# A decoder layer in split fp32: the gate's steps over four blocks, gate rows unsplit, the second norm by a diagonal, the up pass tile by tile

## The chip, the cores and the metric

One core of a Trainium2 chip runs the whole program. The time is device microseconds of one execution; lower is better. TensorE (PE) multiplies matrices, VectorE (DVE) and ScalarE (ACT) work elementwise, GpSimd (POOL) fills buffers and issues some DMAs, SyncE (SP) issues the weights' DMAs.

## The reference, cut to what matters

One layer for 256 tokens of width 2048, all in float32. The vector `c` gives six rows or columns of modulation by a 2048 x 12288 product.

```python
mod = (c_act @ w_mod[l] + b_mod[l])[:, None, :]
sh_m, sc_m, g_m, sh_f, sc_f, g_f = jnp.split(mod, 6, axis=-1)
h = rmsnorm(x, mix_pre_w[l]) * (1 + sc_m) + sh_m
y = hybrid_mixer(h, w_in[l], conv_w[l], gate_w2[l], gate_b[l], gla_norm_w[l], w_out[l])
x = x + g_m * rmsnorm(y, mix_post_w[l])
h = rmsnorm(x, ffn_pre_w[l]) * (1 + sc_f) + sh_f
y = conv_ffn(h, w_up[l], ffn_conv_w[l], w_down[l])
x = x + g_f * rmsnorm(y, ffn_post_w[l])
```

The mixer projects `h`, runs a short convolution and a gated linear attention whose decay is `log_sigmoid((a_lr @ gate_w2 + gate_b)) / 16`, summed along the tokens of each chunk of 64, and projects back. `conv_ffn` is an up product to 11264 columns, a convolution along tokens, `silu(g) * val`, and a down product.

## The kernel before

Float32 products are made from two fp32r halves. For each unit of weights (mostly 1 MB) SP issues a DMA into `raw`; ACT casts it to the high half `wh` (`high`, L141); DVE subtracts to get the low half `wl` (`low`, L146). PE does three products: high by high, high weights by low activations, low weights by high activations. There are six `raw` buffers and three each of `wh` and `wl`. Each of the four stages is a list of such units: in-projection (`tail` is its last chunk of 18 units and what follows), out-projection (`owait`), up pass (`s1`, then `s2`), down pass.

`drive` writes all of them out in one order. Each unit has lists of other steps: `early`, then the DMA and cast of the unit two ahead and the low half of the next, then `pre`, the matmuls, `mid`, the finishing steps of the unit before, and `late`. Every engine executes its own part strictly in that order, so a step that waits holds up all behind it on its engine. `hold` moves the cast and the low half of a unit. PSUM has eight banks, given out in the order of release.

Modulation sums are made on DVE step by step (`macc`, L137): one step stands in most units. Then 128-row sums are added up by products with ones: columns (L285) for the norms, rows (L308, L309) for the gates. `split_acc` (L265, L267) first makes high and low halves of the sums in a `wh` and a `wl` buffer; where it is left out the product is true fp32, which PE executes as two instructions.

- Gate chain: `gla_gate0` to `gla_gate2` make the gate's product, absolute value, exponential, logarithm (ACT, L537 to L539), minimum (DVE, L137 on `big`) and the running sums (four scans, L547), placed at `tail[0]` and `tail[1]`.
- Second norm (`second_norm`, `norm_part0`): after the residual, x is scaled by 1/rms on DVE (`scale_part`, L1135, 256, 256 and 512 columns), turned by transposes on PE (L348), scaled and shifted by the modulation (L354, first tile L1150 and L1151), and split into high (L363) and low (L367) as `h2[0]` to `h2[3]`, two k-blocks each. `h2[4]` to `h2[7]` follow within the up pass.
- Up pass: a group is 512 of the 11264 columns, four column tiles in four PSUM banks. `s1` takes k-blocks 0 to 7 of ten groups (20 units of four k-blocks), `s2` the rest: k 8 to 15 of these ten and all of the other twelve (68 units). In a unit the loop over k is outside and that over column tiles inside; each step is a pair of matmuls of 512 and 256 columns (L874, L876). The first two k-blocks of the first unit are done apart (L868). Finished groups are copied by ACT (L797) and summed by DVE (L799).
- The second modulation's sums `f2` are split at `s1[13]`, its products stand at `s1[14]` and `s1[15]`.

Of the kernel before, what the change touches and what calls it, by code (L numbers as in the profile page):

```python
# [34 lines left out]
LWS = 1  # L35
ORD = (0, 5, 1, 6, 2, 7, 3, 8, 4, 9, 10)
# [7 lines left out]
F2_AT = (70, 74, 13)  # L44
# [25 lines left out]
def drive(units):  # L70
# [5 lines left out]
    for i, u in enumerate(units):  # L76
        for f in u.early:
            f()
        if not u.hold:
            if i + 2 < n:  # L80
                units[i + 2].prep()
            if i + 1 < n:
                units[i + 1].low()
        elif u.hold == 1:
            units[i + 1].low()
# [5 lines left out]
        if u.hold:  # L91
# [13 lines left out]
def layer_kernel(ctx: ExitStack, tc, x, c, w_mod, b_mod, mix_pre_w, mix_post_w, w_in, conv_w, gate_w2, gate_b,  # L105
# [187 lines left out]
    def mod_rows(accs, post, tiles):  # L293
# [240 lines left out]
    def gla_gate1():  # L534
# [186 lines left out]
    def z_part(t, n, ps):  # L721
# [4 lines left out]
        square_sum(ps, ssy[t][:, n:n + 1])  # L726
# [9 lines left out]
    def out_units(nh):  # L736
# [7 lines left out]
        def unit(k2):  # L744
# [24 lines left out]
            def fin(ts=(0, 1), ns=(0, 1)):  # L769
                for t in ts:  # L770
                    for n in ns:
                        z_part(t, nh * 2 + n, pss[t, n])
# [67 lines left out]
    def up_units(og, ks, mode):  # L840
# [4 lines left out]
        def unit(k0):  # L845
# [11 lines left out]
            def mm():  # L857
# [5 lines left out]
                if apart:  # L863
                    for i in range(3):
                        for kk in range(2):
                            for o in range(4):
                                w, xl, half = ((wh, 0, 0), (wh, 1, 1), (wl, 0, 1))[i]
# [28 lines left out]
    def down_unit(k):  # L896
# [49 lines left out]
        def fin():  # L946
            for t in range(2):
                zs[t][0] = zs[t][1] = None
            for t in range(2):
                for n in range(4):  # L950
                    z_part(t, n, down["ps"][t, n])
# [66 lines left out]
    owait[r0 + R0].late.append(lambda: split_acc(gacc))  # L1018
# [16 lines left out]
    tail[1].early.append(gla_gate1)  # L1035
    tail[1].late.append(gla_gate2)
# [37 lines left out]
    for g in ORD:  # L1074
        for og in (g, g + 11):
            s2 += up_units(og, range(8, 16), "rest") if og in A else up_units(og, range(16), "all")
# [3 lines left out]
    def second_norm():  # L1080
# [13 lines left out]

        products()
# [11 lines left out]
        scale_part(0, 0, r0)  # L1107
        st_f["ps"] = [turn_norm(hx, (k, k + 1), None, (0,)) for k in range(0, 8, 2)]
        r1 = rstd_of(sums[1], 4, "n21")
        scale_part(1, 0, r1)  # L1110
        columns()
        st_f["r"] = [r0, r1]

    def put_away():
        for t in range(2):
            for h in range(2):
                if h:
                    scale_part(t, 1, st_f["r"][t])
# [9 lines left out]
    def scale_part(t, h, r):  # L1128
# [121 lines left out]
```

## Time and profile before

| | |
|---|---|
| Time, median of 3 (lowest to highest) | 1223.4 us (1222.33 to 1223.87) |
| The profiled execution's own time | 1223.4 us |
| Its span | 1221.5 us |
| PE, DVE, ACT busy | 96%, 78%, 47% |
| Mean granted TensorE clock | 0.989 of full speed |
| DMA traffic over the span | 262 GB/s |

The span runs from the first to the last record of the profile. "Busy" adds up the time in which an engine executes. PEclk is the TensorE clock that was granted, 1.00 for its full 2.4 GHz and 0.50 for 1.2 GHz. An entry such as [2.28 <-DVE wl L146] says that the engine was idle for 2.28 us before and what ended this. In a matmul's row `128*128` is the weights' size; the first matmul of a fenced row with a count stands for a run of like ones.

### The profile page before, as it was taken

The page shows a single profiled execution, that of the slowest core. Times are in us where ns is not written, and L with a number is a line of the kernel's source. Part 1 is how long each engine was busy: PE and PEld are TensorE (multiplying, and loading weights), DVE is VectorE, ACT ScalarE, POOL GpSimd, SP SyncE. Part 2 cuts the span into 40 slices and gives each one's busy share as a digit, 9 for nine tenths or more (in the row PEclk, how much of TensorE's full clock was granted, in tenths as well). Part 3 has the DMA queues.
Part 4 walks back from the last instruction along what each step waited for, and adds up shares of the span by engine and source line. Part 5 has one row for each costly group of instructions (what it writes and reads, how often), then busy time and mean ns, then how long its engine had stood idle before and what let it go on. Part 6 is the DMA issues. An engine that isn't in the chain of part 4 may idle for free.

```text
span 1221.5 us, 17082 instructions
## 1 busy us (share of the span) xinstructions
PE 1174.3 (96%) x6977; PEld 1043.0 (85%) x6977; DVE 955.2 (78%) x973; ACT 572.9 (47%) x668; POOL 31.7 (3%) x49
## 2 busy tenths in 40 slices
PE   2999999999999998999999999999999999999997
PEld 1999999989997787888888888888888888888885
DVE  5999999989998879974787979798885665444464
ACT  5553432443565437444554555454545543433441
POOL 2000020000001001000000000000000000000000
PEclk9999999999999998998999999999999999999999
DMA  9999999987599995995575776758664665555522
GB/s 306 386 390 385 311 358 394 397 284 254 190 324 347 336 343 205 383 360 169 180 268 202 250 277 208 275 206 278 239 234 150 249 246 189 207 178 201 195 81 69
DMA packets 128046, 320.73 MB, mean 263 GB/s; under 512 B 8341, under 2 KB 35685, under 8 KB 118240
## 3 DMA queue, kind: packets, MB, share of 16 engines
q1 hardware_dynamic: 125360, 312.63, 71.9%
q0 software_dynamic: 2320, 6.94, 1.6%
q8 instruction: 55, 0.90, 0.3%
q14 instruction: 23, 0.19, 0.0%
q10 hardware_dynamic: 288, 0.07, 0.0%
HBM read 315.42 MB, written 4.19 MB: 262 GB/s over the span
## 4 chain that ended last, share of the span: by engine, by line
PE 54%; DVE 0%; ACT 0%; DVEq 0%; issue 0%; ACTq 0%
PE ps L874 22%; PE ps L876 11%; PE ps L733 7%; PE ps L734 7%; PE ps L732 7%; PE ps L285 0%; DVE big L137 0%; PE ps L348 0%; PE ps L308 0%; PE ps L309 0%; ACT junk L335 0%; DVE big L727 0%; DVEq L1234 0%; DVE big L799 0%; ACT rz L321 0%
## 5 line engine op out<-in xcount | busy, mean ns | idle before, releaser
L141 ACT CAST wh<-raw 128x2048 fp32r<-128x2048 f32 (+3 forms) x202 | 366.2, 1816 | 500.2 <-PE ps L874 163.5
L146 DVE TENSOR_TENSOR wl<-raw,wh 128x2048 fp32r<-128x2048 f32 (+3 forms) x202 | 437.7, 2168 | 137.1 <-ACT wh L141 137.1
L874 PE MATMUL ps<-big,wh 128*128 128x512 f32 x1400 | 490.2, 394 | 0.0
L876 PE MATMUL ps<-big,wl 128*128 128x256 f32 x1400 | 393.3, 281 | 0.0
L874 PEld LDWEIGHTS ps<-big,wh 128*128 128x128 f32 x1400 | 263.4, 188 | 59.3
L876 PEld LDWEIGHTS ps<-big,wl 128*128 128x128 f32 x1400 | 265.8, 190 | 0.0
L479 PE MATMUL ps<-big,wl 128*128 128x256 f32 x733 | 210.7, 287 | 4.6 <-DVE wl L146 4.6
L477 PE MATMUL ps<-big,wh 128*128 128x256 f32 x733 | 211.9, 289 | 0.2 <-ACT wh L141 0.2
L478 PE MATMUL ps<-big,wh 128*128 128x256 f32 x733 | 209.9, 286 | 0.0
L137 DVE SCALAR_TENSOR_TENSOR macc<-raw,c_act,macc 128x2048 f32<-128x2048 f32 (+1 forms) x96 | 199.4, 2077 | 3.7 <-DMA raw<-in_w_mod_dram 3.6
L733 PE MATMUL ps<-wl,big 128*128 128x512 f32 x456 | 177.8, 390 | 3.6 <-DVE wl L146 3.6
L732 PE MATMUL ps<-wh,big 128*128 128x512 f32 x456 | 177.9, 390 | 0.0
L734 PE MATMUL ps<-wh,big 128*128 128x512 f32 x456 | 177.5, 389 | 0.0
L479 PEld LDWEIGHTS ps<-big,wl 128*128 128x128 f32 x733 | 143.1, 195 | 5.8 <-DVE wl L146 5.7
L477 PEld LDWEIGHTS ps<-big,wh 128*128 128x128 f32 x733 | 143.4, 196 | 2.7 <-PE ps L423 1.3
L478 PEld LDWEIGHTS ps<-big,wh 128*128 128x128 f32 x733 | 143.3, 196 | 0.1
L733 PEld LDWEIGHTS ps<-wl,big 128*128 128x128 f32 x456 | 85.6, 188 | 22.4 <-DVE wl L146 4.8
L732 PEld LDWEIGHTS ps<-wh,big 128*128 128x128 f32 x456 | 85.6, 188 | 17.8
L734 PEld LDWEIGHTS ps<-wh,big 128*128 128x128 f32 x456 | 85.6, 188 | 17.6
L137 DVE SCALAR_TENSOR_TENSOR big<-big,fcw,big 128x254 f32<-128x254 f32 (+1 forms) x176 | 72.2, 479 | 0.0
L799 DVE TENSOR_TENSOR big<-big,ps 128x256 f32<-128x256 f32 x88 | 31.1, 416 | 43.5 <-ACT big L797 43.5
L819 ACT ACTIVATE big<-big,fcw 128x256 f32<-128x256 f32 x88 | 37.8, 512 | 14.1 <-DVE big L810 14.1
(183 smaller groups left out, 686.9 us busy)
## 6 DMA issues: line engine op xcount, KB each, us to landing
raw<-in_w_up_dram SPq DMA_DIRECT2D x88, 1024.0 KB, 5.3
raw<-in_w_mod_dram SPq DMA_DIRECT2D x64, 1024.0 KB, 7.1
raw<-in_w_down_dram SPq DMA_DIRECT2D x44, 1024.0 KB, 4.8
raw<-in_w_in_dram SPq DMA_DIRECT2D x24, 960.0 KB, 8.3
raw<-in_w_mod_dram SPq DMA_DIRECT2D x32, 640.0 KB, 7.8
raw<-in_w_out_dram SPq DMA_DIRECT2D x16, 1024.0 KB, 7.0
raw<-in_w_in_dram SPq DMA_DIRECT2D x12, 1024.0 KB, 8.0
raw<-in_w_mod_dram SPq DMA_DIRECT2D x22, 512.0 KB, 6.7
```

The costliest lines, as they stand in the source:

```text
L137: nc.vector.scalar_tensor_tensor(o, a, s, b, op0=op0, op1=op1)
L141: nc.scalar.copy(hi, raw)
L146: nc.vector.tensor_sub(lo, raw, hi.bitcast(F32))
L477: nc.tensor.matmul(ps, w[0][:, kk, cs], ht[:, k % 2, 0, :], start=st, stop=False)
L478: nc.tensor.matmul(ps, w[0][:, kk, cs], ht[:, k % 2, 1, :], start=False, stop=False)
L479: nc.tensor.matmul(ps, w[1][:, kk, cs], ht[:, k % 2, 0, :], start=False, stop=sp)
L732: nc.tensor.matmul(ps, a[:, i, 0, ts_], w[0][:, kk, ns], start=st, stop=False)
L733: nc.tensor.matmul(ps, a[:, i, 0, ts_], w[1][:, kk, ns], start=False, stop=False)
L734: nc.tensor.matmul(ps, a[:, i, 1, ts_], w[0][:, kk, ns], start=False, stop=sp)
L819: nc.scalar.activation(st["c"][:, o, :], st["u"][o], AF.Copy, scale=fcw[:, 2, ch + o:ch + o + 1])
L874: nc.tensor.matmul(pss[o], wh[:, kk, cs], h2[k // 2][:, k % 2, :, :], start=(first and kk == 0), stop=False)
L876: nc.tensor.matmul(pss[o][:, 1, :], wl[:, kk, cs], h2[k // 2][:, k % 2, 0, :], start=False, stop=(last and kk == 3))
```

## The change

- The gate's steps become `gla_gate0` to `gla_gate4` and are spread from `tail[0]` to `tail[3]`: the exponential at the end of `tail[1]`, the logarithm at the start of `tail[2]`, the minimum at its end, the scans at the start of `tail[3]`.
- The first gate's sums (`gacc`) and `f2` are no longer split; their products are true fp32. `split_acc` remains for the second gate.
- The first half of x is no longer scaled. DVE multiplies the identity by 1/rms (`diagonal`), and PE multiplies x by it (`turn_scaled`), in true fp32. The last quarter's second half is turned behind the first up unit's matmuls; the second up unit's cast and low half stand behind the first two quarters.
- In a unit of the up pass the loop over column tiles is outside, that over k inside. `apart` takes high, low weights, low activations. `s2` begins with a whole group (5), and the order of groups is written out.
- `f2`'s steps reach `s1[15]`, its products stand at `s1[16]` and `s1[17]`; `h2[4]` to `h2[7]` are turned from `s1[17]` to `s2[1]`.
- The squares and the products with the gate's row of an out tile take turns between two banks.

```diff
-LWS = 1
-ORD = (0, 5, 1, 6, 2, 7, 3, 8, 4, 9, 10)
+ORD = (5, 0, 11, 16, 1, 12, 6, 17, 2, 13, 7, 18, 3, 14, 8, 19, 4, 15, 9, 20, 10, 21)
...
-            hi, lo = accs[1]
+            terms, r = (accs[1], ones_r) if len(accs) == 2 else ((accs[0],), ones)
             for q in range(2):
                 s, cs = slice(q * 512, (q + 1) * 512), slice(h * 1024 + q * 512, h * 1024 + (q + 1) * 512)
                 ps = bank([P, 512])
-                nc.tensor.matmul(ps, ones_r, hi[:, cs], start=True, stop=False)
-                nc.tensor.matmul(ps, ones_r, lo[:, cs], start=False, stop=True)
+                for j, term in enumerate(terms):
+                    nc.tensor.matmul(ps, r, term[:, cs], start=j == 0, stop=j == len(terms) - 1)
                 nc.vector.tensor_mul(parts[h][:, s], ps, parts[h][:, s])
...
         nc.scalar.activation(kb, qb, AF.Exp, scale=-1.0)
+
+    def gla_gate2():
+        qb, kb = gla["qk"]
         nc.scalar.activation(qb, kb, AF.Ln, bias=ones[:, 0:1])
 
-    def gla_gate2():
-        b, (qb, kb) = gla["b"], gla["qk"]
+    def gla_gate3():
+        qb, kb = gla["qk"]
         for hh, ps in enumerate(gla["z"]):
             hs = slice(hh * 2, hh * 2 + 2)
             stt(kb[:, hs, :], ps, 0.0, qb[:, hs, :], ALU.min, ALU.subtract)
+
+    def gla_gate4():
+        b, (qb, kb) = gla["b"], gla["qk"]
         for h in range(HEADS):
...
-                for kk in range(2 * apart, 4):
-                    k = k0 + kk
-                    for o in range(4):
+                for o in range(4):
+                    for kk in range(2 * apart, 4):
+                        k = k0 + kk
...
-    owait[r0 + R0].late.append(lambda: split_acc(gacc))
...
-    tail[1].early.append(gla_gate1)
-    tail[1].late.append(gla_gate2)
+    tail[1].late.append(gla_gate1)
+    tail[2].early.append(gla_gate2)
+    tail[2].late.append(gla_gate3)
+    tail[3].pre.append(gla_gate4)
...
+        def diagonal(t, r):
+
+            if t == 0:
+                st_f["dg"] = slot([P, 2, P])
+            st_f["d", t] = d = st_f["dg"][:, t, :]
+            nc.vector.tensor_scalar_mul(d, ident, r)
...
-        scale_part(0, 0, r0)
-        st_f["ps"] = [turn_norm(hx, (k, k + 1), None, (0,)) for k in range(0, 8, 2)]
+        diagonal(0, r0)
+        columns()
+        st_f["ps"] = [bank([P, 2, T]) for _ in range(4)]
+        for j in range(4):
+            turn_scaled(j, 0)
         r1 = rstd_of(sums[1], 4, "n21")
-        scale_part(1, 0, r1)
-        columns()
+        diagonal(1, r1)
         st_f["r"] = [r0, r1]
+
+    def turn_scaled(j, t):
+        for i in range(2):
+            k = j * 2 + i
+            nc.tensor.matmul(st_f["ps"][j][:, i, t * P:(t + 1) * P], xs[t][0][:, k * P:(k + 1) * P], st_f["d", t],
+                             start=True, stop=True)
...
     def norm_part0():
-        for j in range(4):
-            turned(0, j)
-            used(0, j)
-            if j == LWS:
-                s1[1].low()
-
-    owait[-1].hold, s1[0].hold = 1, 2
+        for j in range(3):
+            turn_scaled(j, 1)
+        used(0, 0)
+        used(0, 1)
+        s1[1].prep()
+        s1[1].low()
+        used(0, 2)
+
+    def norm_part1():
+        turn_scaled(3, 1)
+        used(0, 3)
+
+    owait[-1].hold, s1[0].hold = 3, 2
...
+    s1[0].mid.append(norm_part1)
...
-    s1[13].late.append(lambda: split_acc(f2))
-    s1[14].late.append(lambda: f_products(0))
-    s1[15].mid.append(lambda: f_products(1))
-    s1[15].mid.append(lambda: later["c"][2]())
-    for j in range(4):
-        at = 16 + 2 * (j // 2)
-        s1[at].late.append(lambda j=j: turned(1, j))
-        s1[at + 1].pre.append(lambda j=j: used(1, j))
+    s1[16].late.append(lambda: f_products(0))
+    s1[17].mid.append(lambda: f_products(1))
+    s1[17].mid.append(lambda: later["c"][2]())
+    for j, u in enumerate((s1[18], s1[19], s2[0], s2[1])):
+        (s1[17].late if j == 0 else u.early).append(lambda j=j: turned(j))
+        u.pre.append(lambda j=j: used(1, j))
```

DVE around the gate, before. `macc` is a modulation step, `big_2600` the gate's minimum, L547 the scans, `wl` the low halves of the coming blocks:

```order
L137 SCALAR_TENSOR_TENSOR macc_1922<-raw_2607,c_act,macc_1922 128x2048
L146 TENSOR_TENSOR wl_2618<-raw_2543,wh_2545 128x1920
L137 SCALAR_TENSOR_TENSOR big_296<-ps_2549,big_296 128x512
L137 SCALAR_TENSOR_TENSOR big_2600<-ps_2601,big_2599 128x512
L137 SCALAR_TENSOR_TENSOR big_2600<-ps_2604,big_2599 128x512
L547 SCALAR_TENSOR_TENSOR big_2598<-reset,big_2600 128x256 x4
L137 SCALAR_TENSOR_TENSOR macc_1922<-raw_2673,c_act,macc_1922 128x2048
L146 TENSOR_TENSOR wl_2680<-raw_2614,wh_2616 128x1920
```

DVE at the same place in the changed kernel:

```order
L136 SCALAR_TENSOR_TENSOR macc_1922<-raw_2607,c_act,macc_1922 128x2048
L145 TENSOR_TENSOR wl_2614<-raw_2543,wh_2545 128x1920
L136 SCALAR_TENSOR_TENSOR big_296<-ps_2549,big_296 128x512
L136 SCALAR_TENSOR_TENSOR macc_1922<-raw_2666,c_act,macc_1922 128x2048
L145 TENSOR_TENSOR wl_2674<-raw_2610,wh_2612 128x1920
L136 SCALAR_TENSOR_TENSOR big_296<-ps_2580,big_296 128x512
L402 TENSOR_TENSOR big_335<-big_335,ps_2631 128x512
L136 SCALAR_TENSOR_TENSOR big_2600<-ps_2601,big_2599 128x512
L136 SCALAR_TENSOR_TENSOR big_2600<-ps_2604,big_2599 128x512
L136 SCALAR_TENSOR_TENSOR macc_1922<-raw_2727,c_act,macc_1922 128x2048
L145 TENSOR_TENSOR wl_2732<-raw_2670,wh_2672 128x1280
L552 SCALAR_TENSOR_TENSOR big_2598<-reset,big_2600 128x256 x4
```

A modulation step and a low half (`wl_2674`) now stand ahead of the minimum steps, and one more of each ahead of the scans.

ACT around the second modulation sums, before: L141 casts weights, L265 casts the sums, L797 copies a finished group out of its banks:

```order
L141 CAST wh_5056<-raw_5054 128x2048
L265 CAST wh_5092<-macc_4094 128x1024 x2
L141 CAST wh_5100<-raw_5098 128x2048
L797 COPY big_5140<-ps_5009 128x256
L797 COPY big_5140<-ps_5010 128x256
L797 COPY big_5140<-ps_5011 128x256
L797 COPY big_5140<-ps_5012 128x256
```

ACT at the products' new place in the changed kernel (L140 casts weights, L805 copies):

```order
L140 CAST wh_5132<-raw_5130 128x2048
L140 CAST wh_5170<-raw_5168 128x2048
L805 COPY big_5210<-ps_5082 128x256
L805 COPY big_5210<-ps_5083 128x256
L805 COPY big_5210<-ps_5084 128x256
L805 COPY big_5210<-ps_5085 128x256
L140 CAST wh_5231<-raw_5229 128x2048
```

No cast of sums stands between the weights' casts and the copies.

PE from the end of the first up unit to the second, before. `ps_4424` to `ps_4427` are the four banks, `big_4403` is `h2[1]`, `big_4413` `h2[2]`, `wh_4387` the second unit's weights:

```order
L874 MATMUL ps_4426<-big_4403,wh_4231 128x512
L876 MATMUL ps_4426<-big_4403,wl_4247 128x256
L874 MATMUL ps_4427<-big_4403,wh_4231 128x512
L876 MATMUL ps_4427<-big_4403,wl_4247 128x256
L874 MATMUL ps_4424<-big_4413,wh_4387 128x512
L876 MATMUL ps_4424<-big_4413,wl_4406 128x256
L874 MATMUL ps_4425<-big_4413,wh_4387 128x512
L876 MATMUL ps_4425<-big_4413,wl_4406 128x256
L874 MATMUL ps_4426<-big_4413,wh_4387 128x512
L876 MATMUL ps_4426<-big_4413,wl_4406 128x256
```

PE at the same place in the changed kernel, where `big_4400` is `h2[2]` and `big_4452` `h2[3]`:

```order
L882 MATMUL ps_4406<-big_4388,wh_4223 128x512
L884 MATMUL ps_4406<-big_4388,wl_4239 128x256
L882 MATMUL ps_4406<-big_4388,wh_4223 128x512
L884 MATMUL ps_4406<-big_4388,wl_4239 128x256
L1135 MATMUL ps_4357<-big_4350,big_3947 128x128 x2
L882 MATMUL ps_4403<-big_4400,wh_4393 128x512
L884 MATMUL ps_4403<-big_4400,wl_4395 128x256
L882 MATMUL ps_4403<-big_4400,wh_4393 128x512
L884 MATMUL ps_4403<-big_4400,wl_4395 128x256
L882 MATMUL ps_4403<-big_4452,wh_4393 128x512
L884 MATMUL ps_4403<-big_4452,wl_4395 128x256
```

The turning of the last quarter stands between the units, and the first bank takes `h2[3]` after two pairs, where before all four banks took `h2[2]` first.

## Rows read from the trace of the kernel before

**Rows 1.** The page, part 1: busy us (share of the span) xinstructions of each engine.
```profile
PE 1174.3 (96%) x6977; PEld 1043.0 (85%) x6977; DVE 955.2 (78%) x973; ACT 572.9 (47%) x668; POOL 31.7 (3%) x49
```

**Rows 2.** Windows: us, busy us (xinstructions) of five engines, PEclk, DMA share, GB/s.
```profile
251.28:262.18 10.90, 10.90 (x91) 10.90 (x91) 7.61 (x9) 8.22 (x7) 0.00 (x0) 1.00 0.59 210
262.18:271.61 9.43, 7.15 (x48) 6.95 (x46) 9.43 (x8) 1.81 (x1) 0.00 (x0) 0.82 0.82 278
457.15:481.14 23.99, 20.90 (x121) 18.38 (x120) 20.98 (x30) 19.10 (x35) 3.84 (x5) 0.79 0.45 161
481.14:548.98 67.84, 67.84 (x386) 58.80 (x385) 58.02 (x47) 29.49 (x36) 0.00 (x0) 1.00 1.01 375
554.80:568.14 13.34, 10.61 (x49) 9.51 (x49) 3.62 (x5) 2.95 (x5) 0.00 (x0) 0.74 0.67 225
644.00:710.56 66.56, 66.56 (x386) 58.69 (x385) 58.67 (x75) 33.47 (x38) 0.00 (x0) 1.00 0.72 251
```

**Rows 3.** Timeline, gate chain: start us, us, engine, operation, count [idle before <-releaser].
```profile
256.86 1.29 DVE L137 SCALAR_TENSOR_TENSOR big<-ps,big 128x512 f32<-128x512 f32 x2 [3.29 <-ACT big L539]
...
262.65 2.15 DVE L146 TENSOR_TENSOR wl<-raw,wh 128x1920 fp32r<-128x1920 f32 x1
...
264.86 0.43 PE L479 MATMUL ps<-big,wl 128*128 128x256 f32 x1 [2.28 <-DVE wl L146]
```

**Rows 4.** Timeline, out-projection around the gate rows.
```profile
381.98 1.91 ACT L141 CAST wh<-raw 128x2048 fp32r<-128x2048 f32 x1
...
386.04 1.91 ACT L265 CAST wh<-macc 128x2048 fp32r<-128x2048 f32 x1 [2.15 <-issue]
...
387.99 2.29 DVE L267 TENSOR_TENSOR wl<-macc,wh 128x2048 fp32r<-128x2048 f32 x1 [3.82 <-ACT wh L265]
...
391.24 0.39 PE L308 MATMUL ps<-wh,ones_r 128*128 128x512 f32 x1
...
393.11 0.40 PE L732 MATMUL ps<-wh,big 128*128 128x512 f32 x1
393.24 2.29 DVE L146 TENSOR_TENSOR wl<-raw,wh 128x2048 fp32r<-128x2048 f32 x1
395.58 0.50 PE L733 MATMUL ps<-wl,big 128*128 128x512 f32 x1 [2.08 <-DVE wl L146]
...
405.24 0.50 PE L733 MATMUL ps<-wl,big 128*128 128x512 f32 x1 [1.16 <-DVE wl L146]
```

**Rows 5.** Timeline, PE alone: fp32 matmuls of 128 and 256 columns.
```profile
305.11 1.95 PE L566 MATMUL ps<-big 128*128 128x128 f32 x16
306.89 6.64 PE L474 MATMUL ps<-hf,raw 128*128 128x256 f32 x30
313.37 1.95 PE L566 MATMUL ps<-big 128*128 128x128 f32 x16
```

**Rows 6.** Timeline, second norm, DVE, GpSimd (POOL) and ACT.
```profile
462.40 3.07 DVE L1135 TENSOR_SCALAR big<-big,n 128x256 f32<-128x256 f32 x3
...
463.10 1.82 POOL L171 MEMSET macc<- 128x2048 f32 x1
...
466.09 1.01 DVE L1135 TENSOR_SCALAR big<-big,n 128x256 f32<-128x256 f32 x3
...
469.91 0.69 DVE L367 TENSOR_TENSOR big<-hf,big 128x512 fp32r<-128x512 f32 x1
...
470.76 1.01 ACT L354 ACTIVATE hf<-ps,ash 128x256 f32<-128x256 f32 x2
...
471.81 0.62 ACT L363 CAST big<-hf 128x512 fp32r<-128x512 f32 x1
```

**Rows 7.** Timeline around the products of the second modulation columns.
```profile
549.07 2.00 ACT L265 CAST wh<-macc 128x1024 fp32r<-128x1024 f32 x2 [3.42 <-PE ps L874]
...
556.96 1.41 DVE L799 TENSOR_TENSOR big<-big,ps 128x256 f32<-128x256 f32 x4 [2.25 <-ACT big L797]
557.53 0.24 PE L285 MATMUL ps<-ones_r,wh 128*128 128x2 f32 x1 [2.73 <-DVE big L799]
```

More of the change, by code (lines that the diff above doesn't have):

```diff
@@ L43 @@
 MODS = (10, 21, 31, 46, 70)
-F2_AT = (70, 74, 13)
+F2_AT = (70, 75, 16)
 FULL = (5, 9, 13)
@@ L83, in drive @@
                 units[i + 1].low()
-        elif u.hold == 1:
+        elif u.hold == 3:
             units[i + 1].low()
@@ L90, in drive @@
             f()
-        if u.hold:
+        if u.hold in (1, 2):
             units[i + 2].prep()
@@ L719, in layer_kernel, with z_square, z_value @@
     gpw = [None, None]
-    def z_part(t, n, ps):
+    def z_square(t, n, ps):
+        square_sum(ps, ssy[t][:, n:n + 1])
+    def z_value(t, n, ps):
         if zs[t][n // 2] is None:
@@ L767, in mm, with fin @@
                     block(k, t)
-            def fin(ts=(0, 1), ns=(0, 1)):
+            def fin(ts=(0, 1)):
                 for t in ts:
-                    for n in ns:
-                        z_part(t, nh * 2 + n, pss[t, n])
+                    for n in range(2):
+                        z_square(t, nh * 2 + n, pss[t, n])
+                        z_value(t, nh * 2 + 1 - n, pss[t, 1 - n])
             return Unit(prep, lows, mm, [fin] if k2 == 7 else [])
@@ L866, in mm @@
                             for o in range(4):
-                                w, xl, half = ((wh, 0, 0), (wh, 1, 1), (wl, 0, 1))[i]
+                                w, xl, half = ((wh, 0, 0), (wl, 0, 1), (wh, 1, 1))[i]
                                 nc.tensor.matmul(pss[o][:, half, :], w[:, kk, o * P:(o + 1) * P],
                                                  h2[0][:, kk, xl, :], start=(kk == 0 and i == 0), stop=False)
-                for kk in range(2 * apart, 4):
-                    k = k0 + kk
-                    for o in range(4):
+                for o in range(4):
+                    for kk in range(2 * apart, 4):
+                        k = k0 + kk
                         cs = slice(o * P, (o + 1) * P)
@@ L950, in fin @@
                 for n in range(4):
-                    z_part(t, n, down["ps"][t, n])
+                    z_square(t, n, down["ps"][t, n])
+                    z_value(t, n ^ 1, down["ps"][t, n ^ 1])
                 finish_row(t)
@@ L1073, in layer_kernel @@
     s2 = []
-    for g in ORD:
-        for og in (g, g + 11):
-            s2 += up_units(og, range(8, 16), "rest") if og in A else up_units(og, range(16), "all")
+    for og in ORD:
+        s2 += up_units(og, range(8, 16), "rest") if og in A else up_units(og, range(16), "all")
     hx = [[None, None], [None, None]]
@@ L1117, in put_away @@
                 if h:
-                    scale_part(t, 1, st_f["r"][t])
+                    scale_part(t, st_f["r"][t])
                 away[t, h] = dram.tile([P, 1024], F32, tag=f"away{t}{h}", name=f"away{t}{h}")
@@ L1126, in fetch, with scale_part, turned @@
                 nc.gpsimd.dma_start(xs[t][h], away[t, h])
-    def scale_part(t, h, r):
-        hx[t][h] = slot([P, 1024])
-        if h:
-            nc.scalar.activation(hx[t][h], xs[t][h], AF.Copy, scale=r)
-        else:
-            for s in (slice(0, 256), slice(256, 512), slice(512, 1024)):
-                nc.vector.tensor_scalar_mul(hx[t][h][:, s], xs[t][h][:, s], r)
-    def turned(i, j):
-        k = i * 8 + j * 2
-        st_f[i, j] = (turn_norm(hx, (k, k + 1), st_f["ps"][j], (1,)) if i == 0 else turn_norm(hx, (k, k + 1)))
+    def scale_part(t, r):
+        hx[t][1] = slot([P, 1024])
+        nc.scalar.activation(hx[t][1], xs[t][1], AF.Copy, scale=r)
+    def turned(j):
+        k = 8 + j * 2
+        st_f[1, j] = turn_norm(hx, (k, k + 1))
     def used(i, j):
-        k, ps = i * 8 + j * 2, st_f[i, j]
+        k, ps = i * 8 + j * 2, st_f[i, j] if i else st_f["ps"][j]
         hf = hf_tile()
@@ L1147, in used @@
             ash = st_f[0]
-            for e in range(2):
-                a, b = ash[:, 8 + e:9 + e], ash[:, e:e + 1]
+            ab = [(ash[:, 8 + e:9 + e], ash[:, e:e + 1]) for e in range(2)]
+            for e, (a, b) in enumerate(ab):
                 nc.scalar.activation(d[:, e, 0, :], ps[:, e, :], AF.Identity, bias=b, scale=a)
+            for e, (a, b) in enumerate(ab):
                 nc.vector.tensor_scalar(hf[:, e, :], ps[:, e, :], a, b, op0=ALU.mult, op1=ALU.add)
```

1 line of the change is left out of this document (removed).

## The prediction

> **What bounds the kernel now.** I read the page's busy table first: TensorE (PE) is busy 1174.3 of 1221.5 us, VectorE (DVE) 955.2 [rows 1]. So the time is PE's stream, and a change is worth what it takes out of PE's idle or slow time; what other engines save counts only where PE waits for them. Next come the windows [rows 2], block by block. In the up pass twelve blocks take 67.84 us (5.65 each, 0.353 per pair of matmuls) in its first stage and 66.56 us (5.55 each, 0.347 per pair) in its second, both at full clock and with PE busy throughout: nothing waits there. Three stretches are worse: the block at 262.18 takes 9.43 us where two like it take 10.90 together; the seam from 457.15 to 481.14 has a mean clock of 0.79; the stretch from 554.80 to 568.14 has 0.74 and 2.73 us of idle PE. The timeline then tells what PE waits for there: a low half of the weights that DVE subtracts late [rows 3], the same twice in the out-projection [rows 4], the second norm [rows 6], and a bank that DVE empties late [rows 7]. The change touches all four. The profiled execution took 1223.4 us, 1.9 more than its span, and that is also the median; I work against the span and add 1.9.
>
> **Gate chain over four blocks.** Before, DVE comes to the gate's minimum step and sits 3.29 us until ScalarE (ACT) has done its logarithm; behind it in DVE's queue stand the four scans, a modulation step and the subtraction that makes the next block's low half, which so starts at 262.65; PE stops 2.28 us for it [rows 3], and the clock of that window is 0.82 [rows 2]. In the new order the modulation step and the subtraction stand ahead of the gate's steps. The 3.29 us are no longer ahead of the subtraction, nor are the minimum steps (1.29); even with the wait alone gone it starts at 262.65 − 3.29 = 259.36 and ends 2.15 later, at 261.5, before PE asks at about 262.2. The excess of the block is 9.43 − 10.90 / 2 = 3.98 [rows 2]: idle time and the half clock that follows it. The logarithm has a whole block before its reader, the scans now stand behind the following low half, and the first reader of what they make keeps its place five rows on in DVE's order, so I see no new wait. Gain 4.0; if DVE, which had no idle time in that block (9.43 busy of 9.43), is late by as much again, it is 0. I take 4.0.
>
> **Gate rows unsplit.** Before, a cast (1.91 us) and a subtraction of the gate's sums stand in the queues of ACT and DVE, and DVE idles 3.82 us for the cast; the weights' cast that had been ready since 383.9 gets its low half only from 393.24 on. PE stops 2.08 and 1.16 us for the lows [rows 4]. Both split steps go, and the buffers of the weight rings that they held, so the lows come 4 to 6 us earlier and both stops should go: from start to start the first cost 395.58 − 393.11 − 0.23 = 2.24, and 1.16 more make 3.40. On the other side the eight single-pass matmuls (1.87 us from 391.24 to 393.11) become four fp32 products of 512 columns, two PE instructions each. No such shape is in the trace. By 30 fp32 instructions of 256 columns in 313.37 − 306.89 = 6.48 us, 0.216 each, and 16 of 128 columns in 1.78 us, 0.111 each [rows 5], 512 columns are 0.42 (bounds 0.216 and 0.45), so 8 × 0.42 = 3.4, or +1.5 (bounds −0.1 and +1.7). Net −1.9.
>
> **The seam.** Removed: six multiplications of x by its scale on DVE. One of them ran into GpSimd's memset: the first three take 3.07 us together, the same three later 1.01 [rows 6]. Added: two 128-column multiplications that make diagonals (0.25 to 0.35 each), and turning by true fp32 products: 32 PE instructions where 16 transposes were, at 0.111 [rows 5] or twice that at half clock, which this window has for (1 − 0.79) / 0.5 × 23.99 = 10 us [rows 2]. Moved: the cast of the second up block and its low behind the first two quarters, ACT's two first high halves ahead of DVE's, and the last quarter's turning behind the first up block.
> Worked forward: the first diagonal at 462.4 as the scaling now, PE from 462.7, 16 × 0.222 = 3.55 to 466.3. The second is ready by then, since DVE no longer loses 2 us. If the clock rises here: 12 × 0.111 to 467.6, ACT's two high halves (1.01) by 467.8, the first up block at 467.95; its 24 matmuls at 0.121 to 470.85, where the low ones no longer wait, eight pairs to 473.7, the last quarter 0.44 to 474.1. Its activation, cast and subtraction take 1.01 + 0.62 + 0.69 [rows 6], 2.4 with the handovers, so it is ready at 476.5. Tile by tile, the second block needs it after two pairs, at 474.85: a new PE wait of 1.65 us. Then 14 pairs, 4.95, to 481.4. If the clock rises only at 469.9, the same chain ends at 482.9. Before it is 481.14, so +0.3 to +1.8: I take +1.0. Full clock throughout brings the first up block 1.15 us forward, the term to −0.8; a first diagonal held until the memset ends (463.10 + 1.82 [rows 6]) is ready 2.4 us later, +4.2 on the late clock. Both are the term's bounds.
> By the row, the scaling behind its first instruction lost 2 us while GpSimd's memset ran. The Trainium skill ("SBUF — State Buffer", section "Who interferes with whom") says that a tensor-scalar operation in its two-port mode and GpSimd share a pair of ports, and whichever issues first keeps the other out for its whole length. The trace agrees (3.07 against 1.01 us). By that rule the new diagonal is safe only if it issues ahead of GpSimd; with it behind, the sum would be 1215.8 and not 1212.6.
> The squares and products of each out tile are interleaved; each pair still reads its two banks one engine after the other. Zero here and in the end of the kernel.
>
> **Second modulation columns unsplit and later.** Before, ACT casts the sums twice at 549.07 (after 3.42 us of waiting for a weight buffer), which pushes the next weight cast, the copies of the finished group and DVE's sum of it to 556.96; the products need its bank and PE stops 2.73 us, then runs at half clock [rows 7]. Now no cast stands in ACT's queue, and the products run two blocks later on the sums themselves, again 16 PE instructions. Needed: a block of 5.65 and 16 × 0.111 = 1.78, together 7.4; taken: 13.34 [rows 2]. Gain 5.9; it is 0 if another holder of the bank keeps the products waiting. The group's copies and sums that free the bank stand ahead of the products by nearly a block of PE's work, and only the casts had pushed them to its end.
>
> **Up pass tile by tile, one group first.** Same count of matmuls: 1400 pairs. Four pairs in one bank follow each other instead of one pair per bank. I set this to 0: within a pair two matmuls already share a bank at this pace, and the in-projection runs many in one bank (10.90 us for 90 matmuls [rows 2]). Turning the second half of k in two-tile pieces is the same count of transposes. With four activations between, their bank reads end before the tile that needs the bank.
>
> Sum: −4.0 − 1.9 + 1.0 − 5.9 = −10.8; span 1210.7, time 1212.6 us.
>
> **Rivals.**
> *The pace of the pairs.* It is 0.353 in the first stage and 0.347 in the second [rows 2], with no wait in either, so it is set by how the stream restarts after other work, and the change alters every restart. If the 68 units of the second stage run at the slow pace, 68 × 0.106 = +7.2: 1219.8 us. The 20 first ones at the fast pace would give −2.1: 1210.5. For it: both are seen. Against it: the fast one holds in all twelve blocks of its window.
> *One bank costs more (slower than before).* If a pair that follows a pair into the same bank loses a second step of 6.6 ns over the slow pace, 0.360 per pair, the 312 pairs of the first stage lose 2.1 us and the 1088 of the second, at 13.3 ns, 14.4: 1212.6 + 16.5 = 1229.1. It decides from 10.8 us / 1400 = 7.7 ns per pair. Against it are the in-projection's rows.
> *DVE takes it back.* DVE is full in the block of the gate [rows 2]; if the lows come late again, by the gate and in the out-projection, 4.0 + 3.4 return: 1220.0.
> *The change does not do what it says.* If another holder of the bank keeps the products waiting, the 5.9 stay: 1218.5.
>
> **How the numbers follow.** The forecast has 0.52, with a range of its own of 1209 to 1216 from the seam's bounds. The slow pace has 0.25, DVE 0.09, the unchanged stop 0.08, the one bank 0.06. A measurement can tell 0.2%, 2.4 us, from no change: below 1221.0 is faster, above 1225.8 slower. The first case lies wholly below, the slow pace and the unchanged stop nearly so, DVE's case half: faster 0.86, same 0.08, slower 0.06. The range goes from 1208 (the first stage fast, the seam's better bound) to 1220.5.
>
> **What would show it.** The block before the last of the gate takes 5.4 to 5.5 us and no PE wait on a low half stands there; in the out-projection eight fp32 instructions take about 3.4 us and the waits of 2.08 and 1.16 are gone; in the seam the diagonals take under 0.4 us, and the second up block shows a wait of 1 to 2 us after its second pair for the last quarter; around the products no idle PE and no half clock; pairs at 0.347 in the second stage. It is wrong if pairs there run above 0.354, if the seam is over 28 us, or if the products still wait.

## The result, and the profile after

The changed kernel takes 1219.4 us (median of 20 runs, 1215.2 to 1224.6), the kernel before in the same runs 1225.0 (1222.3 to 1235.4); the ratio is 0.9942, 95% interval 0.9924 to 0.9961. That is faster by 0.6% by the ratio and by 0.5%, 5.6 us, by the medians; it is within the stated range, and about half of the forecast gain of 10.8. The profiled execution took 1220.7 us, its span is 1218.9.

The windows of the changed kernel that answer to [rows 2]: the gate's blocks (two and one), the seam, its second block alone, fifteen blocks of the first stage, the two products with the block between, twelve blocks of the second stage.

```profile
252.75:263.64 10.89, 10.89 (x91) 10.89 (x91) 10.89 (x10) 6.78 (x7) 0.00 (x0) 1.00 0.99 335
263.64:269.05 5.41, 5.41 (x48) 5.41 (x47) 5.41 (x7) 1.80 (x1) 0.00 (x0) 1.00 0.99 337
452.30:479.46 27.16, 23.32 (x137) 21.64 (x136) 17.99 (x26) 19.18 (x35) 3.94 (x5) 0.81 0.43 153
470.20:479.46 9.26, 7.47 (x35) 6.25 (x34) 7.28 (x4) 7.33 (x7) 0.00 (x0) 0.82 0.69 227
479.46:562.66 83.20, 83.20 (x482) 73.36 (x481) 69.00 (x59) 37.39 (x47) 0.00 (x0) 1.00 0.93 341
562.66:571.80 9.14, 9.14 (x66) 8.39 (x65) 0.36 (x1) 3.51 (x2) 0.00 (x0) 1.00 0.34 117
601.66:669.50 67.84, 67.84 (x387) 58.84 (x386) 57.44 (x81) 35.24 (x41) 0.00 (x0) 1.00 0.70 239
```

The block at 263.64 now takes 5.41 us at full clock (9.43 before), and DVE is busy all through both windows without a wait. Around the products there is no idle PE and no low clock. The first stage runs at 83.20 / 15 = 5.55 us per block, the second at 67.84 / 12 = 5.65: the two paces of [rows 2] have changed places.

The timeline of DVE at the gate, where [rows 3] had a wait of 3.29 us:

```profile
255.91 2.14 DVE L145 TENSOR_TENSOR wl<-raw,wh 128x1920 fp32r<-128x1920 f32 x1
...
259.18 1.27 DVE L136 SCALAR_TENSOR_TENSOR big<-ps,big 128x512 f32<-128x512 f32 x2
260.38 2.33 DVE L136 SCALAR_TENSOR_TENSOR macc<-raw,c_act,macc 128x2048 f32<-128x2048 f32 x1
262.64 1.47 DVE L145 TENSOR_TENSOR wl<-raw,wh 128x1280 fp32r<-128x1280 f32 x1
264.04 2.42 DVE L552 TENSOR_TENSOR_SCAN big<-reset,big 128x256 f32<-128x256 f32 x4
```

The low half of the block at 263.64 is ready at 258.05, 5.6 us ahead. PE around the gate rows, which answers to [rows 4]:

```profile
388.70 3.59 PE L308 MATMUL ps<-macc,ones 128*128 128x512 f32 x8
391.73 0.79 PE L739 MATMUL ps<-wh,big 128*128 128x512 f32 x1
392.36 0.39 PE L740 MATMUL ps<-wl,big 128*128 128x512 f32 x1
```

The eight fp32 instructions start 0.43 us apart. The matmul behind them is recorded as starting at 391.73, but the next one starts only 0.63 us later, where such a step usually takes 0.23; so the eight take 392.36 − 388.70 − 0.23 = 3.43 us. No row behind them waits. The stretch from the gate rows through the three units behind them, first in the kernel before, then in the changed one:

```profile
391.24:413.33 22.09, 18.85 (x81) 14.86 (x80) 18.99 (x13) 7.92 (x5) 1.46 (x2) 1.00 0.84 312
388.70:408.48 19.78, 19.78 (x82) 15.03 (x80) 14.47 (x10) 5.74 (x3) 2.35 (x2) 1.00 0.97 371
```

The seam, as [rows 6]: the first diagonal (DVE), GpSimd's memset, the second diagonal, the turning (PE), and the wait in the second block.

```profile
457.63 0.29 DVE L1109 TENSOR_SCALAR big<-ident,n 128x128 f32<-128x128 f32 x1
457.98 6.32 PE L1135 MATMUL ps<-big,big 128*128 128x128 f32 x28 [2.05 <-DVE big L1109]
458.34 1.82 POOL L170 MEMSET macc<- 128x2048 f32 x1
460.16 0.29 DVE L1109 TENSOR_SCALAR big<-ident,n 128x128 f32<-128x128 f32 x1
463.97 1.28 PE L876 MATMUL ps<-big,wh 128*128 128x256 f32 x8
...
472.93 0.49 PE L882 MATMUL ps<-big,wh 128*128 128x512 f32 x1 [1.79 <-DVE big L366]
```

Both diagonals take 0.29 us; the turning runs at half clock throughout (28 instructions in 463.97 − 457.98 = 5.99 us). The second block waits 1.79 us after its second pair, and its window above has a clock of 0.82.
The first diagonal issued at 457.63, ahead of GpSimd's memset at 458.34, and the second behind it at 460.16 as the memset ended. The Trainium skill ("SBUF — State Buffer", section "Who interferes with whom") makes the order of issue decide who is kept out; here neither diagonal ran beside the memset, so this trace does not test it.

ACT, DVE and PE at the products, as [rows 7]:

```profile
557.20 1.91 ACT L140 CAST wh<-raw 128x2048 fp32r<-128x2048 f32 x1 [3.59 <-PE ps L882]
559.01 1.18 ACT L805 COPY big<-ps 128x256 f32<-128x256 f32 x4
559.40 1.42 DVE L807 TENSOR_TENSOR big<-big,ps 128x256 f32<-128x256 f32 x4 [3.47 <-ACT big L805]
...
562.66 1.84 PE L284 MATMUL ps<-ones,macc 128*128 128x2 f32 x16
```

DVE's sums, which free the banks, end at 560.82, 1.8 us ahead of the products; before, they began at 556.96 and PE stood waiting for them. From the start of the block ahead to the end of the second products the kernel before takes 20.86 us, the changed one 14.7 (557.1 to 571.8):

```profile
548.98:569.84 20.86, 18.12 (x98) 16.00 (x97) 8.18 (x8) 6.56 (x8) 1.08 (x2) 0.84 0.46 154
```

Where 1221.5 − 1218.9 = 2.6 us came from, stretch by stretch, by the starts of the same steps in the two traces: the blocks just ahead of the gate +1.5; gate −4.0; gate rows and the three units behind −2.3 (19.78 us against 22.09); seam +3.2 (27.16 against 23.99); products and the block between −6.1; first stage −1.6 (15 × 0.106); second stage +6.5 (61 × 0.106). The sum is −2.8; the rest is small change.

The +1.5 is no work of the change. Both traces reach the column products at 229.1 us together. Behind these products, twenty matmuls of two columns, the granted clock was 0.66 from 231.30 to 236.30 in the changed kernel's execution and 1.00 in that of the kernel before; up to the gate they then took 23.64 and 22.16 us. Seven of the fourteen profiles have this fall of the clock; the kernel before has it in `before_again` and not in its first profile, so it is part of what spreads the times of one kernel.

### The profile page after: what moved, and what is told of

It reads as the page before. It is cut to its first block, busy times and chain, and to the rows that moved or that the text cites. A ratio compares the mean times of both kernels' runs of the same rounds, so it can differ in the third digit from the quotient of the medians.

```text
span 1218.9 us, 17103 instructions
## 1 busy us (share of the span) xinstructions
PE 1178.1 (97%) x6993; PEld 1043.1 (86%) x6993; DVE 947.4 (78%) x966; ACT 569.6 (47%) x665; POOL 31.9 (3%) x49
## 4 chain that ended last, share of the span: by engine, by line
PE 94%; DMA 3%; DVE 2%; issue 1%; ACT 0%; SPq 0%; DVEq 0%; ACTq 0%
PE ps L882 27%; PE ps L884 14%; PE ps L741 9%; PE ps L740 9%; PE ps L739 9%; PE ps L476 7%; PE ps L478 7%; PE ps L477 7%; DMA raw<-in_w_mod_dram 2%; PE ps L571 1%; PE ps L473 1%; DVE big L136 1%; PE ps L284 1%; PE ps L422 1%; PE ps L1135 1%
## 5 line engine op out<-in xcount | busy, mean ns | idle before, releaser
L140 ACT CAST wh<-raw 128x2048 fp32r<-128x2048 f32 (+3 forms) x202 | 366.3, 1815 | 507.1 <-PE ps L882 195.3
L402 DVE TENSOR_TENSOR big<-big,ps 128x512 f32<-128x512 f32 x66 | 43.2, 678 | 1.5 <-PE ps L478 1.5
```

What stands on the lines that cost most here:

```text
L140: nc.scalar.copy(hi, raw)
L402: nc.vector.tensor_add(dst, dst, ps)
```

## The experiments

Two questions stood open: what makes the pace of the pairs, which costs 5 of the missing 8 us, and why the seam got dearer by 3.2. The theory on the pace: it is drawn (set, by chance or not) when PE's stream of pairs restarts after other work, and is then kept. The rival: the tile-by-tile order makes the second stage slow. "First stage" and "second stage" below are the units free of other PE work in a profile.

| kernel | first stage, us per unit | second stage | median us (runs) |
|---|---|---|---|
| before, first profile | 5.65 | 5.55 | 1225.0 (20) |
| before_again | 5.65 | 5.65 | 1236.6 (1) |
| changed, first profile | 5.55 | 5.65 | 1219.4 (20) |
| same | 5.65 | 5.65 | 1219.9 (12) |
| same2 | 5.55 | 5.65 | 1219.1 (6) |
| kout2 | 5.55 | 5.65 | 1219.8 (11) |
| koutall | 5.65 | 5.65 | 1219.7 (4) |
| regroup1 | 5.65 | 5.65 | 1219.4 (4) |
| gateback | 5.65 | 5.65 | 1224.2 (12) |
| f2split | 5.65 | 5.65 | 1226.6 (6) |
| grouped | 5.61 | 5.61 | 1217.6 (6) |
| groupedk | 5.61 | 5.61 | 1215.1 (6) |
| grouped16k | 5.57 | 5.57 | 1211.6 (6) |
| before16 | 5.57 | 5.57 | 1219.1 (8) |

**same** (no edit)

> The changed kernel again, unaltered. Theory: the pace of the up pass's pairs (0.347 or 0.353 us) is drawn when PE's stream restarts and is then kept, so it differs between executions; in this profile some of the 48 whole-group units or the 20 first units come out at the other pace than in the first profile (5.55 us in the first stage, 5.65 in the second), and the five times spread by about 7 us. Rival: the tile-by-tile order sets it; then the second stage shows 5.65 us per unit again and the times lie within 2 us of each other.

The first stage came out at the other pace (5.65), the second at 5.65 again; the twelve times spread over 4.9 us, 1218.2 to 1223.1, which is neither the 7 of the theory nor the 2 of the rival. So the first stage's pace differs between executions of one program; on the second stage this run cannot tell theory from rival. Its second block waits too, but at full clock, as its window shows (9.26 us and a clock of 0.82 in the first profile):

```profile
471.14:478.75 7.61, 6.00 (x33) 4.99 (x33) 5.79 (x4) 7.34 (x7) 0.00 (x0) 1.00 0.63 205
```

The 28 runs of the kernel before beside it fall into two halves, 14 at 1222.7 to 1226.2 and 14 at 1229.0 to 1233.1.

**before_again** (the kernel before, no edit)

> The kernel before, unaltered, once more with a profile. Theory A (the restart decides, the same way for one program): first stage 5.65 us per unit, second stage 5.55 us from the unit after the last turning on. If the pace is drawn by chance in each execution, the second stage may show 5.65 us and the time be 6 to 7 us longer, about 1230.

The second case came: the same program that ran its second stage at 66.56 us per twelve units [rows 2] now took 67.84, in this window of the new trace:

```profile
605.61:673.45 67.84, 67.84 (x387) 58.85 (x386) 52.45 (x69) 34.70 (x39) 0.00 (x0) 1.00 0.69 235
```

PE is busy throughout at full clock in both. That is 6.5 to 7 us of the 13 between the two executions; the other 6 were lost before the up pass, 4.6 of them by 139 us. The two groups of times of the kernel before, the 28 runs above, have medians 6.7 us apart, about what the pace is worth; only one profile of each pace was taken, so that every run of the upper group is one at the slow pace is likely and not shown. The share of the upper group (1229 and more) changed from one set of runs to another: 8 of 20 in the first comparison, 14 of 28, 9 of 9, 7 of 10, and 2 of 13. So it is no even draw, and a ratio to the kernel before depends on the set. What sets the share stays open.

**koutall**

```diff
-                for o in range(4):
-                    for kk in range(2 * apart, 4):
+                for kk in range(2 * apart, 4):
+                    for o in range(4):
```

> One edit to the changed kernel: all units of the up pass keep k outside and the column tile inside, as before the change. Theory A (the restart decides): which pace the second stage keeps depends on how PE's stream restarts after the last turning, not on the order of the pairs; then its units may be 5.65 us here too, and the time stays at 1219 to 1221. Theory B (the order decides): four pairs in one bank after each other make the slow pace; then the second stage shows 5.55 us as in the kernel before and the time is 1212 to 1215. In both the wait for the last quarter moves behind eight pairs.

```profile
602.50:670.35 67.85, 67.85 (x387) 58.93 (x386) 57.46 (x81) 35.25 (x41) 0.00 (x0) 1.00 0.70 239
```

Second stage 5.65, times 1218.7 to 1221.6: theory B falls, since this order alone does not bring the fast pace, nor does it in `before_again`. Whether an order makes one pace likelier than the other isn't settled by that. From start to start two units at the last turnings, the turnings included, took 6.41 and 7.57 us here, against 6.0 each tile by tile; in the second PE waits 1.30 us. The tile-by-tile order saves these 2.0 us.

**regroup1**

```diff
...
+                if og == 5 and k0 == 8:
+                    todo = [(o, kk, (i,)) for o in range(4) for i in range(2) for kk in range(4)]
...
```

> One edit to the changed kernel: in a single unit, the first after the last turning is used (the third of the second stage), the four 512-column matmuls of a column tile come first, then the four of 256 columns; every other unit is as in the changed kernel. Theory A (the restart decides): behind this unit the stream restarts from another phase and the pace is drawn again; where it was 5.65 us it may become 5.55 for the following 58 units, 6 us in all. Theory B (the order decides): the following units show 5.65 us as before the edit, time within 1 us of the changed kernel.

The one unit took 5.61, all behind it 5.65, also the five behind the second gate's rows that had 5.55 in the first profile. A new restart gave the slow pace again; one case does not tell A from B. Across the profiles of the changed kernel and its like, the second stage was slow 8 times of 8; across the two of the kernel before once. Why the changed programs get it so regularly stays open. Yet a restart does change the pace: in the other seven of these eight it went from 5.65 to 5.55 behind the second gate's rows (at 940.85 us in the first profile) and stayed there, with nothing else altered in the stream.

**grouped**

```diff
...
                         nc.tensor.matmul(pss[o], wh[:, kk, cs], h2[k // 2][:, k % 2, :, :],
                                          start=(first and kk == 0), stop=False)
+                    for kk in range(2 * apart, 4):
+                        k = k0 + kk
                         nc.tensor.matmul(pss[o][:, 1, :], wl[:, kk, cs], h2[k // 2][:, k % 2, 0, :],
...
```

> One edit to the changed kernel: within a column tile the four 512-column matmuls come first, then the four of 256 columns, in the same bank. Theory: the slow pace belongs to the alternation of 512 and 256 columns; in runs of one shape PE keeps 0.227 and 0.120 us, as in the out-projection and the in-projection, so every free unit takes 5.55 us and the time is 6 us below the changed kernel, 1212 to 1214. Rival (one bank is dearer): adding to one bank eight times in a row costs the same or more, units at 5.65 us or above, time not below the changed kernel's.

Units took 5.61 in both stages, the same from the first to the last, and 1217.6 us. The size was missed (5.55 expected): in runs of four the 512-column matmuls start 0.232 us apart on average and not 0.227. But the two paces are gone, and adding eight times in a row to one bank is no dearer than 5.65, so the rival of the dear bank falls. The changed kernel's own first stage says so too: tile by tile, it took 5.55.

**kout2**

```diff
...
+                if og == 0 and k0 < 8:
+                    todo.sort(key=lambda e: e[1])
...
```

> One edit to the changed kernel: only the first two units of the up pass keep k outside and the column tile inside. Theory: the seam's missed 2.2 us are the clock that falls behind the 1.8 us wait for the last quarter; with k outside the last quarter is needed eight pairs (2.8 us) later, wait and half clock go, and the third unit starts 3.5 us earlier. Rival: the wait only moves behind the eighth pair, or the clock falls for the turning at half speed anyway; the third unit starts less than 1 us earlier.

The third unit started 473.81 − 450.43 = 23.38 us after the seam's start, 3.8 earlier than in the first profile and 1.9 earlier than in `same`. Then it waited for its own low half:

```profile
472.93 2.28 DVE L145 TENSOR_TENSOR wl<-raw,wh 128x2048 fp32r<-128x2048 f32 x1
475.27 0.39 PE L886 MATMUL ps<-big,wl 128*128 128x256 f32 x1 [1.07 <-DVE wl L145]
```

The median is that of `same` to 0.1 us. The wait for the last quarter went, as the theory had it; the theory overlooked what is next in DVE's queue. The clock's fall is no test of it, since `same` had none with the wait in place.

**gateback**

```diff
-    tail[1].late.append(gla_gate1)
-    tail[2].early.append(gla_gate2)
-    tail[2].late.append(gla_gate3)
-    tail[3].pre.append(gla_gate4)
+    tail[1].early.append(gla_gate1)
+    tail[1].early.append(gla_gate2)
+    tail[1].late.append(gla_gate3)
+    tail[1].late.append(gla_gate4)
```

> One edit to the changed kernel: the gate's steps stand where they stood before (exponential and logarithm at the start of the second block, minimum and scans at its end). Theory: DVE waits about 3.3 us for the logarithm again, PE stops about 2.3 us for the low half behind it and runs at half clock after that; the block takes 9.4 us and not 5.4, +4.0 us. Rival: DVE's fullness was the cause, and the block stays under 7 us or the stop moves to another block.

```profile
257.62 1.29 DVE L136 SCALAR_TENSOR_TENSOR big<-ps,big 128x512 f32<-128x512 f32 x2 [4.59 <-ACT big L541]
...
265.62 0.39 PE L478 MATMUL ps<-big,wl 128*128 128x256 f32 x1 [2.27 <-DVE wl L145]
...
363.15 0.50 PE L740 MATMUL ps<-wl,big 128*128 128x512 f32 x1 [1.57 <-DVE wl L145]
```

The window of the block:

```profile
262.94:270.87 7.93, 5.66 (x47) 5.45 (x46) 7.93 (x7) 1.80 (x1) 0.00 (x0) 1.00 0.77 253
```

DVE's wait and PE's stop are back, and the kernel is 4.3 us slower than `same` in medians on the same chip. The composition differs: the block takes 7.93 at full clock, so +2.5 there, and another stop of 1.57 us stands 100 us later, 4.1 together. Between the two DVE is busy 94.3 us of 97, so it has little room to make up for its wait; that this alone brings the second stop is argued, not shown. `before_again` and `before16` have the same pair, 2.27 and 1.6 us, while the first profile of the kernel before lost its 4.0 in the block itself, by the clock, and has no second stop.

**f2split**

```diff
+    s1[15].late.append(lambda: split_acc(f2))
     s1[16].late.append(lambda: f_products(0))
```

> One edit to the changed kernel: the second modulation sums are split into high and low halves again, one unit ahead of the products, which stay at their new place. Theory: the split's cast takes a weight buffer and blocks ACT's queue, the copies and sums that free the bank come late, PE stops about 2.7 us at the products and runs at half clock after that, +5 to +6 us around them. Rival: the new place alone took the stop away; then at most +0.5 us.

```profile
558.91 2.00 ACT L264 CAST wh<-macc 128x1024 fp32r<-128x1024 f32 x2 [3.75 <-PE ps L882]
...
566.76 1.42 DVE L807 TENSOR_TENSOR big<-big,ps 128x256 f32<-128x256 f32 x4 [2.20 <-ACT big L805]
567.33 0.24 PE L284 MATMUL ps<-ones_r,wh 128*128 128x2 f32 x1 [2.73 <-DVE big L807]
```

The same 2.73 us as in [rows 7], at the new place; the two units around the products take 6.2 us more than in `same`. The median is 7.3 us above that of `regroup1` on the same chip, more than the 5 to 6 expected. The split makes the stop, not the place of the products; that it does so through ACT's cast is how the rows read.

**same2** (no edit)

> The changed kernel a third time, unaltered, beside the two regrouped ones. Theory: the pace is drawn per execution, and this program nearly always draws 0.353 us per pair in its second stage; 5.65 us per unit there again, 1218 to 1222 us; against runs of the kernel before that drew the slow pace too (1229 to 1233 us), 11 us less. Rival: the fast pace is as frequent as in the kernel before; then about half of the times lie near 1213.

Second stage 5.65, first 5.55; 1216.7 to 1220.6. The runs of the kernel before beside it took 1223.7 to 1234.7, seven of ten at 1229 or more; their median is 11.4 us above.

**groupedk**

```diff
...
+                todo = [(o, kk, i) for o in range(4) for i in range(2) for kk in range(4)]
+                if og == 0 and k0 < 8:
+                    todo = [(o, kk, i) for kk in range(2 * apart, 4) for o in range(4) for i in range(2)]
...
```

> Two edits to the changed kernel: the first two units keep k outside; all others do the four 512-column matmuls of a column tile first, then the four of 256. Theory: units take 5.61 us whatever the restart (0.04 less than at the slow pace, 68 units, 2.7 us), and the seam loses its wait of 1.8 us for the last quarter; the low half of the third unit, late by 1.1 us with k outside alone, is now asked for 0.9 us later. Together 3 to 5 us below the changed kernel, 1215 to 1217. Rival: the seam gives nothing, as the median of that edit alone; then 1217 to 1218.

1215.1 us, 4.0 below `same2` on the same chip, where `grouped` alone was 2.3 below `same`. The third unit, which with k outside alone (`kout2`) took 6.89 us, takes 6.25 and no longer waits: the low half is asked for later. So removing the seam's wait pays once the low half behind it has time.

**grouped16k**

```diff
...
+                todo = [(o, kk) for o in range(4) for kk in range(2 * apart, 4)]
+                for o, kk in (sorted(todo, key=lambda e: e[1]) if og == 0 and k0 < 8 else todo):
+                    nc.tensor.matmul(pss[o], wh[:, kk, o * P:(o + 1) * P], h2[k // 2][:, k % 2, :, :],
...
+                for o, kk in todo:
+                    nc.tensor.matmul(pss[o][:, 1, :], wl[:, kk, o * P:(o + 1) * P], h2[k // 2][:, k % 2, 0, :],
...
```

> Like the regrouped kernel, but in each unit all sixteen 512-column matmuls stand first, then all sixteen of 256 columns (in the first two units with k outside). Theory: a run of one shape settles at 0.227 and 0.120 us, as in the out-projection and in-projection, after some matmuls at 0.235; units take 5.56 to 5.62 us and the low halves are asked for 3.6 us later, 1213 to 1217. Rival: 512 columns stay at 0.235 in this stage; units take 5.66 to 5.69 us and the time is that of the changed kernel or 1 to 2 us more.

```profile
477.31:555.25 77.94, 77.94 (x451) 68.90 (x449) 68.19 (x55) 36.92 (x45) 0.00 (x0) 1.00 1.00 369
599.52:666.32 66.80, 66.80 (x386) 59.06 (x385) 58.41 (x81) 35.04 (x44) 0.00 (x0) 1.00 0.70 244
```

5.57 us per unit in both stages, and 1211.6 us (1208.7 to 1213.4), 7.6 below `same2` and a ratio of 0.9855 to the kernel before (0.983 to 0.988). It beats both kernels. Two things were altered at once here, the runs of sixteen and the order in the first two units. With two changes of shape per unit the pace is within 0.02 us per unit of the fast one in every unit, and a low half is needed only after the sixteen 512-column matmuls, some 3.6 us into its unit.

**before16** (the kernel before with the same loops)

> The kernel before with one edit: in each unit of the up pass all sixteen 512-column matmuls stand first, then all sixteen of 256 columns (in the first two units with k outside), as in the fastest kernel so far. Theory: this takes the drawn pace out of the kernel before; units take 5.57 us in both stages, its times no longer fall into two groups 7 us apart but lie at 1221 to 1226, and the distance to the changed kernel with the same edit (1211.6) is what the change's other terms are worth, 10 to 13 us. Rival: the two groups have another cause; then times near 1230 are as frequent as in the kernel before, with units at 5.57 us.

The pace is 5.57 in both stages and the eight times lie in 3.5 us, in one group. That fits the theory and is a weak test of it: of the thirteen runs of the kernel before beside it only two were in the upper group, so that another cause of the groups is not ruled out. The median, 1219.1, is below the expected 1221 to 1226, and the distance to grouped16k is 7.5 (on another chip), not 10 to 13. The stop at the products shrank. PE asks for the bank as late as before, 5.7 us behind the start of the block ahead (5.8 in the kernel before), but ACT's first cast of the sums starts 1.7 us ahead of that block (546.72) and not 0.1 behind its start (548.98) as in [rows 7]: the weight buffer that it takes is last read by a 512-column matmul (L873), and those now stand first in their unit:

```profile
545.00 2.00 ACT L265 CAST wh<-macc 128x1024 fp32r<-128x1024 f32 x2 [3.62 <-PE ps L873]
...
553.38 0.24 PE L285 MATMUL ps<-ones_r,wh 128*128 128x2 f32 x1 [0.94 <-DVE big L799]
```

From the start of the block ahead to the end of the second products it takes 15.8 us, where the kernel before took 20.86: 5.1 of the 6 us that the unsplit products gave came from the loops here too. By these numbers, from two chips, the two kernels would differ by an estimated 7.5 + 5.1 = 12.6 us at one pace, near the 10.8 of the prediction.

## Why the prediction was right, and where it failed

**Direction and range** held; the likeliest time, 1212.6, did not come in the median. The forecast's own range, 1209 to 1216, missed. The stated range held because it was drawn wide enough for the first rival: the second stage at the slow pace was to give 1219.8 with a chance of 0.25, and 1219.4 was measured. That the gain still is half of the forecast is in part luck, since the median of the kernel before depends on how many of its runs were in its upper group.

The step that failed is the one that took the pace of the pairs in the kernel before as its own: "the fast one holds in all twelve blocks of its window" was counted against the rival. One program takes either pace: the changed kernel in its first stage (5.55 in its first profile and `same2`, 5.65 in `same`), the kernel before in its second (5.55, and 5.65 in `before_again`). That a restart sets it fits these and the change behind the second gate's rows (`regroup1`); `koutall` shows that the order of the pairs alone does not. Not explained is that the changed kernel's second stage was slow each time: of its 38 times (20, 12 and 6) none is below 1215.2, where the fast pace would put most near 1213.

What I missed is that the kernel before has both paces as well, so that its median of three was one of the better cases. Against the lower of its groups (median 1223.7 of 12 in the first comparison) the change gives 4.2 us; against the upper (1232.0 of 8), which is likely the like pace, 12.6.

**Gate, −4.0:** measured −4.0 in the trace, and 4.3 by undoing it. **Gate rows, −1.9:** −2.3; the fp32 products took 3.43 us by their steps, as the sum had it (3.4), at 0.43 an instruction (0.42), and both stops went.

**Seam, +1.0:** +3.2 in the first profile, but 25.33 and 25.34 us in `same` and `same2`, +1.35, within its +0.3 to +1.8. The wait for the last quarter was 1.65 by the sum and 1.79 and 1.61 in the traces; the turning ran at half clock to its end in the first profile (6.0 us; 6.2 in the late case). The term that the sum lacked is the clock that can fall behind that wait: the second block's matmuls took 7.47 us in the first profile and 6.00 in `same`, so 1.5 us in the one and none in the other.

**Products, −5.9:** −6.1, with `f2split` for the cause. **Tile by tile, 0:** right for the bank (`grouped`, and the first stage at 5.55); that the order saves 2.0 us at the turnings was not foreseen (`koutall`).

**The rivals:** DVE taking the time back did not come, nor did a remaining stop. The dear bank did not come.

## What to carry to other kernels

Before a small gain is summed up, look whether the long stretch that it doesn't touch has one pace or two: twelve blocks of one execution need not hold in the next, and three runs can all be on one side. A stream of unlike matmuls can be rearranged into runs of like ones, which took the two paces away here and moved the need for the late operand back; with the order in the first two units that was worth 7.6 us (`grouped16k`), more than any one of the removed stops. And of a queue that is full, the step behind the one that was late is the next to be late (`kout2`, `gateback`).

## What the hardware showed that was not expected

Alternating fp32r matmuls of 512 and 256 columns hold one of two paces, 0.347 or 0.353 us per pair, at full clock and with no idle time, for hundreds of pairs; the same program took either in different executions. The two are patterns and not noise: at the fast pace every pair takes 0.347 us, at the slow one the starts of the 512-column matmuls lie 0.36, 0.35 and 0.35 us apart in turn, over and over, in every slow stretch looked at (`before_again`, `same`, `kout2`, `koutall` and others). Grouped by four, a pair takes 5.61 / 16 = 0.351 us, by sixteen 0.348, the same in both profiles of each kind.

After a wait of 1.79 us the clock fell to half, from 474.45 to 477.66, in one execution and, after 1.61 us, not in another. Behind the column products at 229 us it fell in seven of fourteen profiles, with no wait of PE.
